# Memory, keys and values of the second block made in front of the first block's experts

## The chip, the cores and the metric

The kernel runs on one core of a Trainium2 chip. The metric is the device time of one execution in microseconds, as the median of several runs. The core's engines are PE (matrix products and transposes), DVE and ACT (element by element work), POOL, and SP, which here only issues loads; ACT and POOL issue loads too. Each engine takes its instructions in the order in which they stand in its own program.

## The reference, cut to what matters

Two blocks follow one another on 256 rows of width 1024, all in 32-bit floats. Of the first block only the second half matters here, of the second block its first lines:

```python
# block 1
x = layer_norm(ALPHA * x + y) * ln1_g + ln1_b            # y: what the mixers gave, through w_out
h = layer_norm(x) * (1 + sc2) + sh2
y = (1 + g2) * hier_moe(h, router_grp_w, router_grp_b, router_exp_w, router_exp_b,
                        exp_w1, exp_w3, exp_w2)           # 32 experts, 2 chosen for each row
x = layer_norm(ALPHA * x + y) * ln2_g + ln2_b
# block 2
p = rms_norm(x, norm_mix_g) @ w_in                        # q is the first part of p
mem_n = rms_norm(mem, norm_mem_g)                         # mem: 256 x 1024, an input
kh, vh = mem_n @ w_mk, mem_n @ w_mv                       # each 256 x 256; don't depend on x
o_att = softmax(q @ kh.T / 8) @ vh                        # by head
```

After that block 2 has its convolution, its RWKV part and 16 experts of its own.

## The kernel before

Rows lie on the 128 partitions in two halves, t = 0 and 1. Block 1's mixers end in `b1_merge` and `b1_out` (product with w_out, residual, moments). `b1_out` frees the tiles of the mixers, opens slots for weights in their place, and starts the stream of the experts: 96 pieces of 2 MB (w1, w3 and w2 of 32 experts), which `fetch` (L1079) loads one after another into nine slots, A0, A1, A2, B0, B1, A3, B2, B3 and S, round and round, on SP's queue. S consists of two halves, which hold LN1's rows `ln1` and the transposed x `HT` until the router is through with them. The first three pieces are fetched in `b1_out`, five in `m1_router`, the ninth behind x's normalization; each later one when the piece nine before it has been used.

`m1_router` (L1100) loads the router's weights into `KmT` and `Vm` (the tiles that later hold block 2's keys and values), its biases into `rbias` and LN1's rows by column into `ln_f`, all in small loads on ACT's queue. `weighted` (L1129) multiplies the weights by four vectors on DVE; `ps_rw` sums them. LN1 and the router's own normalization are folded: `ps_rl` makes the logits from x before LN1 (transposed into HT), and `rlogit` corrects them by means, roots and sums (`rw_col`). Meanwhile DVE normalizes x in place (L1158 and L1159), takes its moments (L138) and roots, ACT writes the normalized rows `z` (L1180), and DVE selects two experts for each row (`sel`). `ps_rank` (L1214) counts the rows ahead of each one, `onehot` places them, `ps_x` (L1276) gathers the rows of four experts, and `ps_h` (L1294) are the first products with the experts' weights.

Behind the last expert `b2_memory` (L1423) loads mem, w_mk and w_mv into slots that the experts have left, transposes mem (`ps_mT`), scales it by column (`nmem`) and makes keys and values (`ps_km`, 32 products with 256 columns). The rows' root mean square is applied later, in `b2_memory_out` (L1459): a product `ps_mr` turns the factors into a row, ACT copies it, DVE multiplies. In between stand LN2 and the mean square of x. Then `b2_in` (L1646) scales x to `z`, transposes it (`ps_z`), ACT and DVE split it into `h_hi` and `h_lo`, and `psd` (L179) is the first product with w_in.

A scheduler that simulates the program puts the instructions of each engine in order. Every load signals its landing on a counter; SP's and ACT's loads go round eight counters, and a load waits in its engine's order until the load before it on its counter has landed. That is the wait DMAHW0 to DMAHW7 in the orders below; POOL's loads go round eight others.

## Time and profile before

| | |
|---|---|
| median of three runs | 1684.29 us (1680.11, 1684.29, 1698.09) |
| profiled execution, its own time | 1693.76 us |
| its span in the trace | 1692.1 us |
| mean granted clock of PE | 0.877 |
| PE / DVE / ACT / POOL busy | 77% / 41% / 20% / 7% |
| bytes read from memory | 507.08 MB |

The span is the profiled execution without what lies around it (1.7 us). The trace counts microseconds from the start of the span. A row of a timeline gives the start, the length, engine, line, operation, what is written and read, and how many instructions were run together; in brackets stands how long the engine sat idle before, and what ended that. SPq and ACTq are the engine's own queue of instructions, in which loads are issued. `wp` is the common name of all the slots' tiles, L62 the line that issues every load. PEclk is the clock that PE was granted, as a share of full speed.

### The profile page before, as it was taken

How to read it: one execution, taken by the hardware profiler on the slowest of the kernel's cores; microseconds unless marked ns; L12 is line 12 of the kernel's file. 1: busy time of each engine (PE TensorE's matmuls, PEld its weight loads, DVE VectorE, ACT ScalarE, POOL GpSimd, SP SyncE). 2: the span in 40 equal slices, each digit the busy share in tenths (PEclk: the TensorE clock that was granted, in tenths of full speed). 3: DMA queues.
4: the chain of work that ended last, by engine and by line, in shares of the span. 5: the costliest groups of instructions: out<-in, count | busy, mean ns of one | idle time of the engine just before them, and what ended most of it. 6: DMA issues, size and time to landing. Idle time of an engine off the chain costs nothing.

```text
span 1692.1 us, 35400 instructions
## 1 busy us (share of the span) xinstructions
PE 1306.0 (77%) x15539; PEld 987.6 (58%) x15539; DVE 695.6 (41%) x1839; ACT 337.3 (20%) x727; POOL 111.4 (7%) x160
## 2 busy tenths in 40 slices
PE   5999999999587775666557998988977766656555
PEld 3898988878565544454435897668853423323222
DVE  4896657687732222122114686465631101001002
ACT  1443433554210000000002453221210000000001
POOL 2122000122000000000000021120000000000000
PEclk9999989899799898898889997675989777878788
DMA  9566578774989999999998611312689999999996
GB/s 330 176 170 143 151 226 259 250 224 166 397 342 424 425 426 426 425 425 426 426 423 309 180 47 35 102 51 94 248 340 422 425 424 426 422 425 425 423 424 263
DMA packets 154947, 513.77 MB, mean 304 GB/s; under 512 B 12319, under 2 KB 118423, under 8 KB 123814
## 3 DMA queue, kind: packets, MB, share of 16 engines
q1 hardware_dynamic: 145152, 499.85, 75.6%
q10 hardware_dynamic: 8886, 10.99, 2.7%
q8 instruction: 124, 2.03, 0.5%
q0 software_dynamic: 752, 0.63, 0.1%
q14 instruction: 33, 0.27, 0.0%
HBM read 507.08 MB, written 2.62 MB: 301 GB/s over the span
## 4 chain that ended last, share of the span: by engine, by line
DMA 49%; PE 37%; DVE 9%; ACT 2%; issue 2%; SPq 1%; POOL 0%; ACTq 0%; DVEq 0%; POOLq 0%
DMA wp<-in_exp_w_dram 21%; PE psd L179 12%; DMA wp<-in_w_e_up_dram 9%; DMA wp<-in_w_e_down_dram 8%; DMA wp<-in_w_e_gate_dram 6%; PE psn L198 4%; PE ps_h L1294 2%; DVE wlo L160 1%; DMA wc<-in_w_in_dram 1%; DMA ada<-in_ada_w_dram 1%; PE ps_x L1276 1%; PE ps_on L880 1%; PE ps_lv L1934 1%; PE ps_cv L1750 1%; SPq L62 1%
## 5 line engine op out<-in xcount | busy, mean ns | idle before, releaser
L2370 PE MATMUL ps_h<-wp,xg 128*32 128x256 f32 x2048 | 160.4, 460 | 98.1 <-DMA wp<-in_w_e_up_dram 57.0
L1294 PE MATMUL ps_h<-wp,xg 128*32 128x128 f32 x4096 | 160.6, 312 | 89.1 <-DMA wp<-in_exp_w_dram 79.9
L1294 PEld LDWEIGHTS ps_h<-wp,xg 128*32 128x32 f32 x4096 | 135.8, 123 | 121.3 <-DMA wp<-in_exp_w_dram 53.8
L2370 PEld LDWEIGHTS ps_h<-wp,xg 128*32 128x32 f32 x2048 | 70.4, 125 | 186.1 <-DMA wp<-in_w_e_up_dram 57.3
L160 DVE TENSOR_TENSOR wlo<-wc,whi 128x1024 fp32r<-128x1024 f32 (+2 forms) x111 | 138.1, 1258 | 49.5 <-ACT whi L159 44.7
L159 ACT CAST whi<-wc 128x1024 fp32r<-128x1024 f32 (+2 forms) x111 | 114.4, 1041 | 141.9 <-PE psd L179 84.0
L179 PE MATMUL psd<-hT_hi,wlo 128*128 128x256 f32 x432 | 124.1, 288 | 3.6 <-DVE wlo L160 3.6
L179 PE MATMUL psd<-hT_hi,whi 128*128 128x256 f32 x432 | 126.1, 292 | 0.0
L179 PE MATMUL psd<-hT_lo,whi 128*128 128x256 f32 x432 | 124.6, 289 | 0.0
L2391 PE MATMUL ps_y<-wp,Vm 128*32 128x256 f32 x960 | 74.8, 470 | 30.5 <-DMA wp<-in_w_e_down_dram 27.4
L1301 DVE SCALAR_TENSOR_TENSOR eu<-eth,ps_h 128x128 f32<-128x128 f32 x32 | 9.2, 286 | 192.7 <-ACT eth L1299 192.7
L179 PEld LDWEIGHTS psd<-hT_hi,wlo 128*128 128x128 f32 x432 | 84.0, 195 | 6.0 <-DVE wlo L160 4.9
L179 PEld LDWEIGHTS psd<-hT_hi,whi 128*128 128x128 f32 x432 | 84.6, 196 | 2.8 <-issue 2.0
L179 PEld LDWEIGHTS psd<-hT_lo,whi 128*128 128x128 f32 x432 | 84.1, 195 | 1.6 <-issue 1.6
L1299 ACT ACTIVATE eth<-ps_h 128x128 f32<-128x128 f32 x32 | 8.9, 277 | 372.0 <-PE ps_h L1294 372.0
L1325 DVE TENSOR_TENSOR ey<-ps_y,mod 32x256 f32<-32x256 f32 x124 | 52.1, 420 | 65.7 <-PE ps_y L1319 64.3
L1319 PE MATMUL ps_y<-wp,egT 128*32 128x256 f32 x992 | 64.5, 401 | 12.8 <-DVE egT L1311 7.3
L2391 PEld LDWEIGHTS ps_y<-wp,Vm 128*32 128x32 f32 x960 | 35.4, 132 | 64.9 <-issue 29.7
L2395 ACT COPY ey<-ps_y 32x256 f32<-32x256 f32 x30 | 10.9, 364 | 289.4 <-DVE ey L2395 289.4
L2395 DVE COPY ey<-ps_y 32x256 f32<-32x256 f32 x30 | 12.5, 418 | 118.5 <-PE ps_y L2391 111.9
L2378 DVE SCALAR_TENSOR_TENSOR KmT<-KmT,ps_h 128x256 f32<-128x256 f32 x16 | 6.7, 422 | 126.8 <-PE ps_h L2370 126.8
L2377 DVE SCALAR_TENSOR_TENSOR KmT<-KmT,ps_h 128x256 f32<-128x256 f32 x16 | 6.7, 422 | 113.1 <-ACT KmT L2375 113.0
(665 smaller groups left out, 2614.2 us busy)
## 6 DMA issues: line engine op xcount, KB each, us to landing
wp<-in_exp_w_dram SPq DMA_DIRECT2D x85, 2048.0 KB, 34.3
wp<-in_w_e_up_dram SPq DMA_DIRECT2D x19, 2048.0 KB, 27.8
wc<-in_w_in_dram SPq DMA_DIRECT2D x35, 1024.0 KB, 5.6
wp<-in_w_e_gate_dram SPq DMA_DIRECT2D x16, 2048.0 KB, 29.0
wp<-in_w_e_down_dram SPq DMA_DIRECT2D x16, 2048.0 KB, 27.0
wp<-in_w_e_down_dram SPq DMA_DIRECT2D x32, 1024.0 KB, 27.1
wp<-in_w_e_gate_dram SPq DMA_DIRECT2D x30, 1024.0 KB, 27.0
wp<-in_w_e_up_dram SPq DMA_DIRECT2D x24, 1024.0 KB, 27.0
```

What stands on the lines that cost most here:

```text
L62: d = (eng or self.nc.sync).dma_start(out=out, in_=in_)
L159: nc.scalar.copy(hi[:, :kk, cs], src)
L160: i = nc.vector.tensor_tensor(lo[:, :kk, cs], src, hi[:, :kk, cs].bitcast(FT), op=OP.subtract)
L179: mm = lambda w, x, st, sp: nc.tensor.matmul(ps[:, c], w, x, start=st, stop=sp, skip_group_check=True)
L198: mm = lambda x, w, st, sp: nc.tensor.matmul(ps[t], x, w, start=st, stop=sp, skip_group_check=True)
L880: mm = lambda t, v, p, st, sp: nc.tensor.matmul(po[:, t], v, p, start=st, stop=sp, skip_group_check=True)
L1294: nc.tensor.matmul(ph[32 * j:32 * j + 32, i].rearrange("p (m c) -> p m c", c=2), xg[:, k, 32 * el:32 * el + 32], v[:, j % 2, j // 2], star ...
L1319: nc.tensor.matmul(py[32 * q:32 * q + 32], gT[j], w2[j][:, 256 * q:256 * q + 256], start=j == 0, stop=j == 3, skip_group_check=True, tile_ ...
L1325: nc.vector.tensor_tensor(Y[32 * el:32 * el + 32, qs], py[32 * q:32 * q + 32], self.g2[32 * el:32 * el + 32, qs], op=OP.mult)
L2370: nc.tensor.matmul(ph[32 * j:32 * j + 32].rearrange("p (m c) -> p m c", c=2), xg[:, 4 * kk + k, 32 * el:32 * el + 32], v[:, j], start=kk + ...
L2391: nc.tensor.matmul(py[32 * q:32 * q + 32], gT[:, c, 32 * j:32 * j + 32], w2[2 * j + c][:, 256 * q:256 * q + 256], start=j + c == 0, stop=j ...
L2395: (nc.scalar.copy if q % 2 else nc.vector.tensor_copy)(Y[32 * el:32 * el + 32, 256 * q:256 * q + 256], py[32 * q:32 * q + 32])
```

## The change

`b1_out` fetches one expert piece in place of three. In front of it `b2_memory_in` takes the first two slots: mem and w_mk go into A0, w_mv and the place for the transposed memory into A1. Its rows are squared on ACT, the roots taken on DVE and the rows scaled on ACT there and then. `m1_router` loads `norm_mem_g` as eight rows, transposes it on PE (`ps_nm`) to have it by column, and makes `ps_mT` and `ps_km` behind the logits; `ps_km` is copied on ACT into KmT and Vm. `ps_km` uses PSUM banks "y" and "x" in place of "h" and "y"; the first four experts' `ps_x` uses bank "x" alone, in place of "x" and "t" by turns. At the end of the experts the loads of the memory, `ps_mT`, `ps_km`, `ps_mr` and DVE's multiplications are gone. The slots' order goes on from two more places.

```diff
@@ -984,8 +984,8 @@
         self.ln1 = self.shaped(self.single("A"), [P, 2, D])
         for i, nm in enumerate(("ln1_g", "ln1_b")):
             self.rows_to_all(self.ln1[:, i], I[nm][0], nc.scalar)
-        for i in range(3):
-            self.fetch()
+        self.b2_memory_in()
+        self.fetch()
         self.close("w1", "ws", "b1t", "b1", "pc", "pd")
 
     def moments_of(self, pool, st, eps, tag):
@@ -1119,6 +1119,12 @@
                                 channel_multiplier=-1)
         self.before = before
         ones = self.ones
+        nm8 = sp.tile([8, P], FT, name="nmem8")
+        self.load(nm8, I["norm_mem_g_2"][0].rearrange("(r p) -> r p", p=P), nc.scalar)
+        pn = self.pm.tile([P, 8], FT, name="ps_nm", tag="x")
+        nc.tensor.transpose(pn, nm8, self.idn[:8, :8])
+        nmem = sp.tile([P, 8], FT, name="nmem")
+        nc.scalar.copy(nmem, pn)
 
         lg1 = sp.tile([P, 2, 8], FT, name="ln1_f")
         for i, nm in enumerate(("ln1_g", "ln1_b")):
@@ -1154,6 +1160,7 @@
             self.transpose_rows(self.pm, x[:, t], HT, t, ("t", "x"), eng=nc.scalar.copy)
             for k in range(8):
                 nc.tensor.matmul(pl[:, t], HT[:, k, t * P:(t + 1) * P], rs_[:, k], start=k == 0, stop=k == 7)
+        self.b2_memory(nmem)
         for t in range(2):
             nc.vector.scalar_tensor_tensor(x[:, t], x[:, t], mv[t][:, 0:1], lnp[:, 0], op0=OP.subtract, op1=OP.mult)
             nc.vector.scalar_tensor_tensor(x[:, t], x[:, t], rs[t], lnp[:, 1], op0=OP.mult, op1=OP.add)
@@ -1267,9 +1274,9 @@
             if el == 0:
                 G = self.one_hot(e)
                 xg = self.mt.tile([P, 8, P], FT, name="xg", tag="xg")
-                n = 4 if e else 2
+                n = 4
                 for c0 in range(0, 8, n):
-                    px = self.pm.tile([P, n, P], FT, name="ps_x", tag="x" if e else "xt"[c0 // 2 % 2])
+                    px = self.pm.tile([P, n, P], FT, name="ps_x", tag="x")
                     for k in range(n):
                         for t in range(2):
                             c = c0 + k
@@ -1349,15 +1356,13 @@
                     self.rows_to_all(r, I[nm][0])
             self.b2_early(e)
         self.inorder = False
-        kv = self.b2_memory()
         mv = [self.moments_of(self.kv, st[t], 1e-5, f"a{t}") for t in range(2)]
         rs = self.rsqrts(self.kv, [m[:, 1:2] for m in mv], ["ar0", "ar1"], self.LN2LAG)
         for t in range(2):
             nc.vector.scalar_tensor_tensor(x[:, t], x[:, t], mv[t][:, 0:1], lnp[0], op0=OP.subtract, op1=OP.mult)
             nc.vector.scalar_tensor_tensor(x[:, t], x[:, t], rs[t], lnp[1], op0=OP.mult, op1=OP.add)
         self.dump("x2", x)
-        self.rsx = self.mean_square(self.kv, x, "nx", self.shaped(self.free[3], [P, D]))
-        self.b2_memory_out(*kv)
+        self.rsx = self.mean_square(self.kv, x, "nx", self.shaped(self.halves(self.slot(self.spare))[0], [P, D]))
 
     E_IF = 29
     LN2LAG = 0
@@ -1366,6 +1371,7 @@
 
         nc, I, tc = self.nc, self.I, self.tc
         n = nc.values_load(self.cnt[0:1, 0:1], min_val=0, max_val=T)
+        self.spare = self.order[self.npiece % len(self.order)]
         HT = self.big([P, 8, T], name="ov_hT")
         ws = self.big([P, 2, 8, P], name="ov_w")
         w2g = self.big([P, 2, D], name="ov_wg")
@@ -1420,52 +1426,43 @@
         if e == 5:
             self.b2_vectors()
 
-    def b2_memory(self):
-
-        nc, sp = self.nc, self.m1
-
-        o = self.order
-        m, (wk, wv), self.free = self.slot(o[8])[0], self.halves(self.slot(o[2])), \
-            self.halves(self.slot(o[0])) + self.halves(self.slot(o[1]))
-        mT = self.free[0]
-        m = m.rearrange("p (t d) -> p t d", t=2)
-        wk, wv, mT = [w.rearrange("p (k n) -> p k n", k=8) for w in (wk, wv, mT)]
+    def b2_memory_in(self):
+
+        nc = self.nc
+        (m, wk), (wv, mT) = [self.halves(self.take()) for _ in range(2)]
+        jk = self.shaped(mT, [P, 2, D])
+        self.mem = m = m.rearrange("p (t d) -> p t d", t=2)
+        self.mem_w = wk, wv = [w.rearrange("p (k n) -> p k n", k=8) for w in (wk, wv)]
+        self.memT = mT.rearrange("p (k n) -> p k n", k=8)
         self.load(m, self.I["mem_2"][0].rearrange("(t p) d -> p t d", p=P))
         for w, nm in ((wk, "w_mk_2"), (wv, "w_mv_2")):
             self.load(w, self.I[nm][0].rearrange("(k p) n -> p k n", p=P))
+        rs = self.mean_square(self.b1, m, "mm", [jk[:, t] for t in range(2)])
+        for t in range(2):
+            nc.scalar.activation(m[:, t], m[:, t], AF.Copy, scale=rs[t])
+
+    def b2_memory(self, nmem):
+
+        nc, m, mT, (wk, wv) = self.nc, self.mem, self.memT, self.mem_w
         for k2 in range(4):
             ps = self.pm.tile([P, 2, T], FT, name="ps_mT", tag="tx"[k2 % 2])
             for a in range(2):
                 k = 2 * k2 + a
                 for t in range(2):
-                    nc.tensor.transpose(ps[:, a, t * P:(t + 1) * P], m[:, t, k * P:(k + 1) * P], self.idn)
+                    i = nc.tensor.transpose(ps[:, a, t * P:(t + 1) * P], m[:, t, k * P:(k + 1) * P], self.idn)
+                    if k + t == 0:
+                        self.tc.keep_in_program_order(i)
             for a in range(2):
                 k = 2 * k2 + a
-                nc.scalar.activation(mT[:, k], ps[:, a], AF.Copy, scale=self.v2["nmem"][:, k:k + 1])
-        out = []
+                nc.scalar.activation(mT[:, k], ps[:, a], AF.Copy, scale=nmem[:, k:k + 1])
         for v in range(2):
-            ps = self.pm.tile([P, 2, T], FT, name="ps_km", tag="hy"[v])
+            ps = self.pm.tile([P, 2, T], FT, name="ps_km", tag="yx"[v])
             for a in range(2):
                 s = slice(a * P, (a + 1) * P)
                 for k in range(8):
                     l, r = (mT[:, k, s], wv[:, k]) if v else (wk[:, k, s], mT[:, k])
                     nc.tensor.matmul(ps[:, a], l, r, start=k + a == 0, stop=k == 7, skip_group_check=True)
-                out.append(ps[:, a])
-
-        rs = self.mean_square(self.kv, m, "mm", self.shaped(self.free[1], [P, D]))
-        pr = self.pm.tile([P, T], FT, name="ps_mr", tag="t")
-        return out, rs, pr
-
-    def b2_memory_out(self, km, rs, pr):
-        nc = self.nc
-        for t in range(2):
-            nc.tensor.matmul(pr[:, t * P:(t + 1) * P], rs[t].to_broadcast([P, P]), self.idn, start=t == 0, stop=True,
-                             skip_group_check=True)
-        row = self.shaped(self.free[2], [P, T])
-        nc.scalar.copy(row, pr)
-        for a in range(2):
-            nc.vector.tensor_tensor(self.KmT[:, a], km[a], row, op=OP.mult)
-            nc.vector.tensor_scalar(self.Vm[:, a], km[2 + a], rs[a], None, op0=OP.mult)
+            nc.scalar.copy(self.Vm if v else self.KmT, ps)
 
     def b2_vector_loads(self):
         I = self.I
@@ -1538,7 +1535,7 @@
             ss = sp.tile([P, 1], FT, name="ms_s", tag=f"{tag}s{t}")
             r = sp.tile([P, 3], FT, name="rs_y", tag=f"{tag}y{t}")
             out.append(r[:, 0:1])
-            nc.scalar.activation(jk, x[:, t], AF.Square, accum_out=ss)
+            nc.scalar.activation(jk[t] if isinstance(jk, list) else jk, x[:, t], AF.Square, accum_out=ss)
             nc.vector.tensor_scalar(ss, ss, 1.0 / D, 1e-6, op0=OP.mult, op1=OP.add)
             yield
             yield from self.rsqrt_steps(ss, r)
```

The scheduler moves instructions with this. On ACT, before, the router's loads stood between the last work of the mixers (`onT_hi`) and the casts of the weights for the merge; this is that place, around `b1_merge`:

```order
L145 CAST onT_hi<-ps_on 128x256 [waits PE_49]
L62 DMA KmT<-in_router_grp_w_dram 128x8x4 [waits DMAHW3_49]
L62 DMA KmT<-in_router_exp_w_dram 128x8x32
L62 DMA rbias<-in_router_grp_b_dram 128x4
L62 DMA rbias<-in_router_exp_b_dram 128x32
L159 CAST whi<-wc 128x1024 [waits PE_49]
L62 DMA ln_f<-in_ln_g_dram 128x8
L62 DMA ln_f<-in_ln_b_dram 128x8 [waits DMAHW0_49]
```

In the change they stand behind the scaling of the memory's rows, after the last cast and the first copies into HT, and behind them come the rest of HT's copies and everything that ACT does in the router:

```order
L1442 ACTIVATE wp<-wp,rs_y 128x1024 [waits DVE_49,Activation_49] x2
L62 DMA KmT<-in_router_grp_w_dram 128x8x4 [waits DMAHW1_49]
L62 DMA KmT<-in_router_exp_w_dram 128x8x32 [waits DMAHW2_49]
L62 DMA rbias<-in_router_grp_b_dram 128x4 [waits DMAHW3_49]
L62 DMA rbias<-in_router_exp_b_dram 128x32 [waits DMAHW4_49]
L62 DMA nmem_4928<-in_norm_mem_g_dram 8x128 [waits DMAHW5_49]
L62 DMA ln_f<-in_ln_g_dram 128x8 [waits DMAHW6_49]
L62 DMA ln_f<-in_ln_b_dram 128x8 [waits DMAHW7_49]
L1127 COPY nmem<-ps_nm 128x8 [waits PE_49]
L1009 COPY wp<-ps_tr 128x4x128 [waits PE_49] x2
L1457 ACTIVATE wp<-ps_mT,nmem 128x256 [waits PE_49,Activation_49]
```

The seven loads moved from ahead of the merge's last casts to behind them; each now waits on one counter, and the counters 1 to 7 are in order those of w_mv and of the first six expert pieces.

On PE, in the router, from the logits to the gather of the first rows, before:

```order
L1156 MATMUL ps_rl<-Vm,wp 128x36 [waits Activation_49]
L1156 MATMUL ps_rl<-Vm,wp 128x36 x3
L1214 MATMUL ps_rank<-sel,before 128x32 [waits DVE_49]
L1215 MATMUL ps_rank<-sel,before 128x32
L1216 MATMUL ps_rank<-sel,ones 128x32
L1222 MATMUL ps_cnt<-sel,ones 1x32 [waits PE_49]
L1222 MATMUL ps_cnt<-sel,ones 1x32
```

And in the change, from the first product of keys and values on:

```order
L1464 MATMUL ps_km<-wp 128x256 [waits DMAHW7_49,DVE_49,Activation_49]
L1464 MATMUL ps_km<-wp 128x256 [waits DMAHW1_49]
L1452 MATMUL ps_mT<-idn,wp 128x128 [waits PE_49,Activation_49]
L1452 MATMUL ps_mT<-idn,wp 128x128 x3
L1464 MATMUL ps_km<-wp 128x256 x6
L1464 MATMUL ps_km<-wp 128x256 [waits Activation_49]
L1464 MATMUL ps_km<-wp 128x256
L1464 MATMUL ps_km<-wp 128x256 [waits Activation_49]
L1464 MATMUL ps_km<-wp 128x256 x21
L1221 MATMUL ps_rank<-sel,before 128x32 [waits DVE_49]
```

All 32 products `ps_km`, with the last four transposes `ps_mT` between them, stand between the logits and `ps_rank`. The first of them waits for the DVE copy `rw_col`, whose bank it takes.

On DVE, in the change, from the router's four multiplications `weighted` to x's normalization (before, the multiplications stood among the splits of the merge, long ahead of this):

```order
L1136 TENSOR_TENSOR Vm<-KmT,sh_3003 128x288 [waits DMAHW2_49,DMAHW1_49]
L1137 TENSOR_REDUCE rw_sum<-Vm 128x36 [waits DVE_49]
L1136 TENSOR_TENSOR KmT<-KmT,sc_3004 128x288
L1137 TENSOR_REDUCE rw_sum<-KmT 128x36 [waits DVE_49]
L1136 TENSOR_TENSOR Vm<-KmT,ln_f 128x288 [waits DMAHW7_49]
L1165 SCALAR_TENSOR_TENSOR x<-x,bn_mv,wp 128x1024 [waits DMAHW5_49,PE_49]
L1137 TENSOR_REDUCE rw_sum<-Vm 128x36 [waits DVE_49]
L1166 SCALAR_TENSOR_TENSOR x<-x,rs_y,wp 128x1024 [waits DMAHW0_49,DVE_49]
```

The third multiplication, which waits for counter 7, the last `ln_f`, moved ahead of x's first operation.

## Rows read from the trace of the kernel before

**Rows 1.** Page: DMA share of 40 slices; the chain that ended last.

```profile
DMA  9566578774989999999998611312689999999996
...
DMA 49%; PE 37%; DVE 9%; ACT 2%; issue 2%; SPq 1%; POOL 0%; ACTq 0%; DVEq 0%; POOLq 0%
```

**Rows 2.** Busy time by stretch (window, length, busy by engine, granted PEclk, DMA share, GB/s).

```profile
445.00:459.00 14.00, 0.12 (x1) 0.12 (x1) 12.92 (x62) 4.11 (x4) 0.00 (x0) 0.51 1.00 422
459.00:465.00 6.00, 5.44 (x30) 5.00 (x34) 2.88 (x15) 0.46 (x1) 0.00 (x0) 0.50 0.96 399
465.00:473.00 8.00, 8.00 (x130) 6.47 (x134) 2.12 (x7) 1.74 (x4) 0.00 (x0) 0.96 0.06 24
520.00:905.00 385.00, 256.27 (x4674) 185.45 (x4668) 82.44 (x240) 20.41 (x56) 1.38 (x5) 0.88 1.01 424
930.00:940.00 10.00, 7.31 (x39) 6.21 (x38) 5.85 (x13) 3.00 (x5) 0.29 (x1) 1.00 1.06 288
```

**Rows 3.** Waits of SP's queue, 520 to 905 (total us, times, longest).

```profile
SPq L62 <- DMA wp<-in_exp_w_dram: 316.2, 79, 6.1
```

**Rows 4.** SP issues (start, length); the issue at 437.64: KB, us to landing.

```profile
430.46 7.51 SPq L62 DMA_DIRECT2D wp<-in_exp_w_dram  x5
...
472.41 2.14 SPq L62 DMA_DIRECT2D wp<-in_exp_w_dram  x2
...
wp<-in_exp_w_dram SPq DMA_DIRECT2D x1, 2048.0 KB, 24.2
```

**Rows 5.** POOL and ACT issuing small loads (idle before and its releaser); one load's landing.

```profile
424.31 0.50 POOL L62 DMA_DIRECT2D raw<-in_iclr_a_dram  x1 [1.66 <-DMA raw<-in_norm_mix_g_dram]
...
401.29 1.06 ACT L159 CAST whi<-wc 128x1024 fp32r<-128x1024 f32 x1 [2.50 <-DMA KmT<-in_router_grp_w_dram]
...
ln_f<-in_ln_g_dram ACTq DMA_DIRECT2D x1, 4.0 KB, 2.7
```

**Rows 6.** The router on DVE, PE and ACT, by timeline.

```profile
408.03 0.45 DVE L1130 TENSOR_TENSOR Vm<-KmT,ln_f 128x288 f32<-128x288 f32 x1
...
410.13 0.68 DVE L1131 TENSOR_REDUCE rw_sum<-Vm 128x36 f32<-128x288 f32 x1
...
443.59 2.48 DVE L1158 SCALAR_TENSOR_TENSOR x<-x,bn_mv,wp 128x1024 f32<-128x1024 f32 x2
445.98 2.48 DVE L1159 SCALAR_TENSOR_TENSOR x<-x,rs_y,wp 128x1024 f32<-128x1024 f32 x2
448.37 2.47 DVE L138 BATCH_NORM_STATS2 bn_st<-x 128x6 f32<-128x512 f32 x4
...
453.13 0.25 DVE L1169 SCALAR_TENSOR_TENSOR rlogit<-rlogit,rs_y,rbias 128x36 f32<-128x36 f32 x1
...
458.61 0.22 DVE L1206 TENSOR_TENSOR sel<-fm_eq 128x64 f32<-128x64 f32 x1
...
458.88 0.64 PE L1214 MATMUL ps_rank<-sel,before 128*128 128x32 f32 x2 [16.00 <-DVE sel L1206]
...
461.24 3.75 PE L1276 MATMUL ps_x<-onehot,mod 128*128 128x128 f32 x16 [0.56 <-DVE onehot L1233]
...
454.24 3.99 ACT L1180 ACTIVATE mod<-x,nmrs,rs_y 128x1024 f32<-128x1024 f32 x2
```

**Rows 7.** End of the stream: PE, ACT, DVE; the 64 records of L1452.

```profile
913.24 3.67 PE L1261 MATMUL acc<-ey,ecw 128*128 128x512 f32 x8
...
922.92 12.68 PE L1452 MATMUL ps_km<-wp 128*128 128x256 f32 x58
...
938.78 0.38 PE L179 MATMUL psd<-h_hi,whi 128*128 128x256 f32 x1 [1.86 <-ACT h_hi L1663]
...
936.09 0.37 ACT L1465 COPY wp<-ps_mr 128x256 f32<-128x256 f32 x1 [7.37 <-PE ps_mr L1462]
...
929.52 0.75 DVE L1652 TENSOR_SCALAR z<-x,rs_y 128x1024 f32<-128x1024 f32 x1
...
L1452 PE MATMUL ps_km<-wp x64: 379/379/454, 920.7 to 935.2; 128*128 128x256 f32 x64
```

## The prediction

> **What bounds the kernel now.** I read the page first, then busy time by stretch, then the waits of the SP queue, then the timelines of single engines around the two places that the change touches. All times are microseconds from the start of the profiled execution.
>
> The page's row of DMA shares stands at 9 through two long runs of slices, and the chain that ended last is 49% DMA [rows 1]. Between 520 and 905 the DMA is busy all the time at 424 GB/s while PE works 256 of 385 us [rows 2]: block 1's experts are a stream, one 2 MB piece per 2.097 MB / 424 GB/s = 4.95 us. A stream like this ends as late as it was held up before, so what counts is when it stands still. It stands still once: from 465 to 473 the DMA share is 0.06 [rows 2]. Nine pieces have been issued by then, one for each slot, and the tenth can be issued only when the first expert product has freed a slot, at 472.41 [rows 4]. What sets that moment is the router: x normalized on DVE from 443.59, statistics, selection until `sel` at 458.61, then PE's `ps_rank`, which had sat idle 16.00 us, `ps_x` at 461.24 and the expert products [rows 6]. So the date to follow is that of the tenth piece.
>
> The second place is the end of this stream. PE works on the memory's keys and values from 920.7 to 935.6 (`ps_km`, 64 records, the last 58 of them in 12.68 us), and block 2's first product `psd` comes at 938.78 [rows 7], although its input `z` was on its way at 929.52 [rows 7].
>
> **The change, part by part.**
>
> *The load in front.* Memory, w_mk and w_mv are 3.15 MB, 7.4 us at 424 GB/s. They take two slots, which before took two pieces (9.9 us), and those pieces come later through the same two slots. Nine expert pieces have been issued in both kernels before the tenth, so the 7.4 us is no further term as long as the tenth is what decides; it is the whole cost if the tenth were not delayed (rivals).
>
> *The router's small loads on ACT's queue.* This is the step on which the forecast rests. Before, they stood ahead of the merge's last casts and one of those casts followed them at 401.29 [rows 5]. Now the order puts them behind the memory's squares and scaling, and each waits for an earlier load on its counter: the router's weights for w_mv and for the first expert piece, the biases for the second and third, `nmem` for the fourth, the last of them (`ln_f`, LN1's bias) for the sixth. The trace shows what such a wait is. SP stood 316.2 us in 79 waits of this kind [rows 3], and POOL, issuing small loads one after another, stood 1.66 us until the load eight earlier had landed [rows 5]. An engine waits in order: ACT's cast at 401.29 came 2.50 us late behind its loads [rows 5]. So ACT stands until the sixth piece has landed, and behind it are queued `nmem`, the copies of the second half of HT, `ps_mT`'s scaling, `gexp` and `z`. On DVE the third `weighted` needs that last `ln_f` and stands ahead of the first `x` operation, so x's normalization waits too.
>
> When is that? Before, the eighth piece was issued at 437.64 and took 24.2 us, so it landed at 461.8 [rows 4]. Now 3.15 MB and six pieces are ahead, in place of eight pieces: 1.05 MB less, 2.5 us earlier, 459.3; but the second expert piece still waits for a DVE operation of the merge, as at 430.46 [rows 4], and the queue can run dry ahead of it. I take 460.5 (459.3 to 461.8). `ln_f` then takes 2.7 us to land, as before [rows 5], and 0.4 to issue: 463.6. POOL's small loads took longer beside full queues, but here nothing else is in flight, since the next piece (the ninth slot's first half) waits for x. At the upper end I allow 3 us more.
>
> *DVE from there.* Two `weighted` (0.45 each, and a reduction of 0.68 behind each), the x operations 2.48 + 2.48, statistics 2.47, reciprocal roots 2.6 (450.8 to 453.4, the last logits), and 0.4 for the router's sums: 12.9 us [rows 6]. That is 476.4, against 453.4 in the profile. From there to `sel` it was 5.2 us (453.4 to 458.61), and some 1.0 more goes to the logits' first four operations, which stood ahead of x before (0.25 each, as at 453.13): 483 [rows 6].
>
> *Keys and values in front of `ps_rank`.* In PE's new order all 32 products stand ahead of `ps_rank`. The first needs the PSUM bank that `rw_col` frees at about 476; the rest need the last scaled transposes, which ACT has queued behind `gexp` and two `z` operations (3.99 us together [rows 6], where the tile goes by `mod`), so they come at about 483 to 485. About eight products fit in before that, 24 are left. One costs two records, 12.68/58 x 2 = 0.437 us, at the full clock [rows 7]: 10.5 us, until 494. The clock is open: PE's granted clock was 0.51 from 445 to 459, when it had nothing to do, and 0.50 until 465 [rows 2], and PE now idles from 443 to about 476. At the half clock throughout it is 32 x 0.874 = 28 us from 476, until 504. I take the full clock for the 24, since PE was back at 0.96 in 465 to 473 after some 7 us of work [rows 2].
>
> *From `ps_rank` to the tenth piece.* Before, 2.4 us to `ps_x` and 11.2 to the issue, at the half clock until 465; without it I take 1.7 and 9. So 494 + 10.7 = 504.7 against 472.4: **+32 us**, between +27 (early landing, K and V done by 490) and +45 (half clock, late landing). The two slots of the memory come free a little before that and are the eighth and ninth piece; they fill part of the hole, but the tenth still waits.
>
> The Trainium skill says ("DMA: Bandwidth & Descriptors", Rules for kernel authors) to issue a DMA early, compute, and wait on its semaphore late. That speaks for this change as a whole; what it would give here is the first rival. The same page (Issuing engines are not separate DMA queues) counts only the sequencer's time for starting a load and calls it usually small; by that alone ACT's seven loads would cost some 4 us. SP's and POOL's rows above disagree: the issuing engine's stand is the length of an earlier transfer.
>
> *The end of the stream.* `ps_km`, `ps_mr` and the row scaling are gone there. ACT waited 7.37 us for `ps_mr` before it made the casts and `h_hi` [rows 7]; without it the path is z (929.52 + 0.75), transposes, `h_hi`, `psd` at about 931.5, in place of 938.78: -7 us. DVE loses the steps of one pair of roots, up to -1.5 more; two of the loads ahead of w_in_2 are gone (2.1 MB, 7 us at the 288 GB/s of 930 to 940 [rows 2]), so weights don't hold it. On the other side PE comes to block 2 colder. -5 to -10, I take **-7**.
>
> *At no cost:* `ps_nm`, the squares of the memory (ACT was free), the junk slot's new place, `ps_x` with one bank in place of two for the first four experts.
>
> Sum: +32 - 7 = **+25 us**. The profiled execution took 1693.8; the median of the three runs is 1684.3, and they lie 18 us apart. On the median's footing I expect **1709**.
>
> **The rivals.**
>
> *A, the other side: the router is not held up.* If ACT's loads ran ahead (their counters free in time), x and the selection keep their dates, K and V fit into PE's 16 us of idle time and the 7.4 us of loading into the 8 us hole at 465. Then the end's gain is left: -7, up to -9: about 1676. For it: hole and idle time are there [rows 2]. Against it: the order's waits name pieces that land after 450. It decides if x's normalization starts before about 448.
>
> *B, the router is late but K and V are cheap.* If landing comes at 457 and PE is warm, the tenth piece is at 490 to 494: +18 to +21, less 7 to 10: +10 to +13, 1695 to 1697, within 1%. Against it: the products cannot begin before `rw_col`.
>
> *C, half clock.* K and V at 0.874 us throughout, and slow small loads: the tenth at 515 to 518, +43 to +45, less 7: 1720 to 1722. For it: the clock row of 445 to 465.
>
> **How the numbers follow.** A difference of 1% is about what a measurement of this kernel can tell, so slower means above 1701, faster below 1667. Forecast (+17 to +31, 1701 to 1715) 0.58, C (up to 1724) 0.17, B 0.14, A 0.11. A's gain is 0.5%, and only its upper part passes 1%: faster 0.04. Same: the rest of A and B, and the forecast's lower edge: 0.21. Slower 0.75. The range reaches from B's lower end to above C, 1692 to 1724, and leaves out A and a little beyond C.
>
> **What would show it.** Right: ACT issues the last `ln_f` after 459 and computes nothing just before; DVE has a wait for `ln_f` of some 15 us and x starts near 464; `ps_rank` stands behind `ps_km` and comes near 494; the DMA is idle in about 460 to 472, again around 480 to 490, and the tenth expert piece is issued near 505; the last piece lands near 937; from `acc` to the first `psd` it is 7 us less than before (913.24 to 938.78 [rows 7]). Wrong: x starting before 450 (A), K and V over by 490 (B), a granted clock of 0.5 through all of them (C), or a first `psd` no nearer to `acc`, when another wait has taken the place of `ps_mr`.

## The result, and the profile after

| | before | after |
|---|---|---|
| median | 1696.85 us (5 runs, 1680.11 to 1698.09) | 1708.39 us (5 runs, 1699.24 to 1712.39) |
| ratio to before | 1 | 1.0114 (95%: 1.0067 to 1.0162), some 19 us (11 to 27) |
| profiled execution, span | 1692.1 us | 1697.5 us |
| granted clock of PE, mean | 0.877 | 0.866 |

The change makes the kernel slower by about 1%. The profiled execution of after is the fastest of its five, so its span stands only 5.4 us above that of before; the stages tell more than the span.

The page of after, DMA share of 40 slices and the chain that ended last (it answers to [rows 1]):

```profile
DMA  9556478775759999999999541302679999999997
...
DMA 22%; PE 16%; DVE 5%; SPq 1%; ACT 1%; issue 1%; ACTq 0%; DVEq 0%
```

A slice is 42 us. In the two slices from about 424 to 508 the share is 7 and 5, where it was 9 and 8, and the long run of nines behind them ends one slice later. Busy time by stretch (window, length, PE, PEld, DVE, ACT, POOL, granted PEclk, DMA share, GB/s; it answers to [rows 2]):

```profile
459.00:465.00 6.00, 3.63 (x13) 2.34 (x13) 5.93 (x9) 1.85 (x5) 0.00 (x0) 0.50 0.01 1
465.00:473.00 8.00, 7.62 (x36) 7.62 (x37) 7.14 (x32) 1.17 (x3) 0.00 (x0) 0.50 0.40 131
473.00:480.00 7.00, 6.44 (x26) 5.30 (x26) 5.37 (x30) 5.02 (x6) 0.00 (x0) 0.63 0.46 152
480.00:485.00 5.00, 5.00 (x25) 4.41 (x24) 1.12 (x8) 0.71 (x4) 0.00 (x0) 1.00 0.00 0
490.00:495.00 5.00, 4.17 (x34) 3.66 (x32) 2.47 (x12) 0.82 (x2) 0.00 (x0) 1.00 0.97 393
520.00:905.00 385.00, 272.97 (x4782) 196.78 (x4777) 85.31 (x250) 22.54 (x61) 0.00 (x0) 0.84 1.01 425
```

The hole of 8 us in [rows 2] has become a stretch of 26 us in which the DMA is idle or half busy. Why, the timelines of ACT and DVE show:

```profile
441.59 13.16 ACTq L62 DMA_DIRECT2D rbias<-in_router_grp_b_dram  x1
...
457.53 0.44 ACTq L62 DMA_DIRECT2D ln_f<-in_ln_b_dram  x1
459.46 0.17 ACT L1127 COPY nmem<-ps_nm 128x8 f32<-128x8 f32 x1 [17.91 <-PE ps_nm L1125]
```

```profile
458.63 0.46 DVE L1136 TENSOR_TENSOR Vm<-KmT,sh 128x288 f32<-128x288 f32 x1 [16.44 <-DMA KmT<-in_router_exp_w_dram]
...
461.08 1.28 DVE L1165 SCALAR_TENSOR_TENSOR x<-x,bn_mv,wp 128x1024 f32<-128x1024 f32 x1
...
481.07 0.22 DVE L1213 TENSOR_TENSOR sel<-fm_eq 128x64 f32<-128x64 f32 x1
...
491.76 0.23 DVE L1225 SCALAR_TENSOR_TENSOR rank<-ps_rank,sel 128x64 f32<-128x64 f32 x1 [9.86 <-PE ps_rank L1223]
```

ACT stands 13.16 us on one small load. DVE waits 16.44 us for the router's weights, which ACT issued at 440.83, ahead of that stand; a second wait of 9.86 us is for PE, busy with keys and values. The weights' load itself was slow. Issues of after between 430 and 465 (KB each, us from issue to landing):

```profile
wp<-in_exp_w_dram SPq DMA_DIRECT2D x3, 2048.0 KB, 20.0
...
KmT<-in_router_exp_w_dram ACTq DMA_DIRECT2D x1, 128.0 KB, 17.7
```

Why it was slow, the packets show in which the loads move (queue: packets, MB, share of the DMA engines' time; q1 carries SP's loads, q10 ACT's). The first two rows are 444 to 454, the last two 456 to 458:

```profile
q1 hardware_dynamic: 292, 4.26, 99.5%
q10 hardware_dynamic: 285, 0.00, 1.6%
...
q10 hardware_dynamic: 1942, 0.16, 73.7%
q1 hardware_dynamic: 48, 0.13, 17.0%
```

ACT's seven loads are 2,672 packets, most of them of 16 or 128 bytes; SP's pieces go in packets of mostly 16 KB. From 444 to 454 about one packet of ACT's went for each one of SP's, some 29 in a microsecond. When SP's last piece was through, 1,942 went in 2 us.

ACT's stand is not the wait for a completion counter that the prediction names. The load ahead on the counter of the load that stood, the second expert piece, had landed at 436.6 by the trace, 5 us before the stand began; the four loads behind it found their counters free too (landed 441.5, 446.4, 451.4 and 456.4; issued 454.8, 455.4, 456.6 and 457.5). What lay ahead of that load were the packets of ACT's first two loads, in its own queue. That the queue had no room for more is likely, but no run shows it.

PE and SP, from there to the tenth piece:

```profile
459.16 0.27 PE L1125 MATMUL ps_nm<-idn,nmem 8*128 8x8 f32 x1 [23.61 <-DMA nmem<-in_norm_mem_g_dram]
...
477.84 13.29 PE L1464 MATMUL ps_km<-wp 128*128 128x256 f32 x60
490.97 0.30 PE L1221 MATMUL ps_rank<-sel,before 128*128 128x32 f32 x2
...
492.49 2.02 PE L1283 MATMUL ps_x<-onehot,mod 128*128 128x128 f32 x16 [0.56 <-DVE onehot L1240]
```

```profile
501.16 2.15 SPq L62 DMA_DIRECT2D wp<-in_exp_w_dram  x2
```

The end of the stream, on PE (it answers to [rows 7]):

```profile
942.91 3.67 PE L1268 MATMUL acc<-ey,ecw 128*128 128x512 f32 x8
...
961.72 0.58 PE L179 MATMUL psd<-h_hi,whi 128*128 128x256 f32 x1
```

From `acc` to the first `psd` it is 18.8 us, where it was 25.5.

**How the traces are compared.** Executions differ ahead of the changed place: the first transpose of x (`ps_tr`) came at 436.41 in the profile of before and at 432.43 in a second profile of the same kernel. So all times below are counted from that transpose, and the span is cut at two more places: the first `psd` of block 2, and the first product of block 2's own router, `ps_rl` with `r_last`. Between these two lies block 2's mixing work (its RWKV part above all), behind them the experts of block 2. Nothing in either part was edited.

| kernel | `ps_rank` | tenth piece | first `psd` | against before | mixing | rest |
|---|---|---|---|---|---|---|
| before | 22.5 | 36.0 | 502.4 | | 287.5 | 465.8 |
| x9, before again | 22.5 | 36.0 | 502.2 | -0.2 | 287.6 | 464.4 |
| after | 58.0 | 68.1 | 528.7 | +26.3 | 275.9 | 459.9 |
| x5, after again | 57.7 | 67.9 | 528.5 | +26.1 | 275.9 | 459.9 |
| x2, before without the memory | 22.5 | 36.0 | 496.3 | -6.0 | 289.8 | 460.6 |
| x4, slot, few products | 26.5 | 36.9 | 499.3 | -3.0 | 276.9 | 460.4 |
| x1, slot | 34.0 | 44.2 | 504.8 | +2.4 | 287.8 | 461.3 |
| x8, slot and POOL | 34.0 | 44.2 | 504.8 | +2.4 | 277.3 | 460.5 |
| x7, slot and order | 35.4 | 45.6 | 506.2 | +3.8 | 286.8 | 460.3 |
| x6, loads on POOL | 41.0 | 51.2 | 511.6 | +9.2 | 276.0 | 459.8 |
| x3, few products | 48.4 | 60.9 | 523.5 | +21.1 | 287.5 | 460.5 |

From the tenth piece to the first `psd` it is 466.4 and 466.2 us in the two profiles of before, and 460.3 to 460.6 in seven of the others (462.4 and 462.6 in x4 and x3). So for those seven the loss at the first `psd` is the delay of the tenth piece less 6 us for the end of the stream.

Up to the first `psd` the change costs 26.3 us. Then two stretches give back 11.6 and 5.9, which leaves 8.8 of this pair of executions.

### The profile page after: what moved, and what is told of

It is laid out like the page before. It is cut to its first block, busy times and chain, and to the rows that moved or that the text cites. A ratio compares the mean times of both kernels' runs of the same rounds, so it can differ in the third digit from the quotient of the medians.

```text
span 1697.5 us, 35396 instructions
## 1 busy us (share of the span) xinstructions
PE 1311.5 (77%) x15536; PEld 983.9 (58%) x15536; DVE 693.5 (41%) x1835; ACT 340.8 (20%) x731; POOL 114.2 (7%) x160
## 5 line engine op out<-in xcount | busy, mean ns | idle before, releaser
L1301 PE MATMUL ps_h<-wp,xg 128*32 128x128 f32 x4096 | 168.3, 319 | 79.9 <-DMA wp<-in_exp_w_dram 66.2
L160 DVE TENSOR_TENSOR wlo<-wc,whi 128x1024 fp32r<-128x1024 f32 (+2 forms) x111 | 141.7, 1289 | 49.8 <-ACT whi L159 43.9
L2388 PE MATMUL ps_y<-wp,Vm 128*32 128x256 f32 x960 | 73.5, 465 | 27.1 <-DMA wp<-in_w_e_down_dram 23.9
L1326 PE MATMUL ps_y<-wp,egT 128*32 128x256 f32 x992 | 75.0, 450 | 14.9 <-DMA wp<-in_exp_w_dram 10.6
L1326 PEld LDWEIGHTS ps_y<-wp,egT 128*32 128x32 f32 x992 | 36.7, 126 | 40.6 <-issue 20.0
L2375 DVE SCALAR_TENSOR_TENSOR KmT<-KmT,ps_h 128x256 f32<-128x256 f32 x16 | 6.7, 421 | 126.8 <-PE ps_h L2367 126.8
```

The costliest lines, as they stand in the source:

```text
L160: i = nc.vector.tensor_tensor(lo[:, :kk, cs], src, hi[:, :kk, cs].bitcast(FT), op=OP.subtract)
L1301: nc.tensor.matmul(ph[32 * j:32 * j + 32, i].rearrange("p (m c) -> p m c", c=2), xg[:, k, 32 * el:32 * el + 32], v[:, j % 2, j // 2], star ...
L1326: nc.tensor.matmul(py[32 * q:32 * q + 32], gT[j], w2[j][:, 256 * q:256 * q + 256], start=j == 0, stop=j == 3, skip_group_check=True, tile_ ...
L2388: nc.tensor.matmul(py[32 * q:32 * q + 32], gT[:, c, 32 * j:32 * j + 32], w2[2 * j + c][:, 256 * q:256 * q + 256], start=j + c == 0, stop=j ...
```

## The experiments

The theory was that of the prediction: the seven small loads, late in ACT's order, hold ACT, and DVE with it; keys and values in front of `ps_rank` hold the tenth piece further. The rivals: the 7.4 us of loading in front, or the products alone, make the loss. In the kernels with the slot edit, line numbers are 9 higher than in after (up to 17 in x7).

**x1: the memory's roots in the slot.** Only the place of four small tiles changes. They leave the pool of the mixers, and the scheduler puts the router's loads back among the merge's casts.

```diff
-        rs = self.mean_square(self.b1, m, "mm", [jk[:, t] for t in range(2)])
+        rs = self.mean_square(Cut(jk[:, 1]), m, "mm", [jk[:, 0], jk[:, 0]])
```

(`Cut` hands out columns of the slot where the pool handed out tiles.)

> One edit to the changed kernel: the memory's roots (and the junk of its squares) lie in the memory's own slot, no longer in the pool of block 1 over which the router's weight tiles are laid. By the order the seven small loads then stand among the merge's casts again; the 32 products for keys and values stay ahead of ps_rank. Theory (late small loads hold the router, and after that the products hold ps_rank): x starts near 440 in place of 461, sel comes near 457, the products end between 470 and 478 since the last scaled transposes wait behind z and PE is cold, the tenth expert piece is issued at 480 to 488 in place of 501.2; time 13 to 21 us less than the changed kernel, 0 to +7 against the kernel before. Rival (the loads don't matter, the 3.1 MB in front do): time as the changed kernel, +19 against before. Rival (products are free once the router is in time): tenth near 469, -7 against before.

Measured: 1688.13 against 1691.36, ratio 0.9993 (0.9956 to 1.0030). The loads are issued from 393 on, x's normalization starts at 435.1, and the products end at 465.5, somewhat earlier than expected:

```profile
397.12 0.36 ACTq L71 DMA_DIRECT2D ln_f<-in_ln_b_dram  x1
```

```profile
453.35 12.35 PE L1473 MATMUL ps_km<-wp 128*128 128x256 f32 x56 [1.55 <-ACT wp L1466]
465.54 0.30 PE L1230 MATMUL ps_rank<-sel,before 128*128 128x32 f32 x2
```

The same 128 KB of weights now land after 2.8 us:

```profile
KmT<-in_router_exp_w_dram ACTq DMA_DIRECT2D x1, 128.0 KB, 2.8
...
q10 hardware_dynamic: 2387, 0.17, 39.1%
```

The second row is ACT's queue from 394 to 398, with nothing of SP's beside it. The tenth piece comes at 475.7, ahead of the expected 480 to 488. At the first `psd`, 23.9 of the 26.3 us are gone with the place of seven loads. That is the larger part of the loss, shown by undoing it.

**x2: before without the memory.** Loads, products and scaling of the memory are left out; keys and values are a constant.

```diff
-        self.load(m, self.I["mem_2"][0].rearrange("(t p) d -> p t d", p=P))
...
+        self.nc.gpsimd.memset(self.KmT, 0.01)
+        self.nc.gpsimd.memset(self.Vm, 0.01)
```

> The kernel before without the memory's part at the end of the experts: mem, w_mk and w_mv are not loaded, nothing of keys and values is made (both tiles are filled with a constant on POOL). So it leaves out the keys and values. Theory: from acc to the first psd 18.5 to 20 us in place of 25.5, and the time is 7 us less than before (5 to 10). Rival (the end of the stream is bound by the weights of w_in_2 or by DVE): no gain.

Measured: ratio 0.9972 (0.9942 to 1.0002), which just reaches 1. The first `psd` comes 6.0 us earlier:

```profile
911.87 3.67 PE L1261 MATMUL acc<-ey,ecw 128*128 128x512 f32 x8
...
930.63 0.58 PE L179 MATMUL psd<-h_hi,whi 128*128 128x256 f32 x1
```

From `acc` to `psd` it is 18.8 us, as in after. So this is all that moving the memory away from the end can bring.

**x3 and x4: 4 of the 32 products**, in after and in x1. The other 28 are left out, so keys and values are sums over an eighth of the columns.

```diff
-                for k in range(8):
+                for k in range(7, 8):
```

> The changed kernel with 4 of the 32 products for keys and values (one of eight parts of the width; the rest of the sum is left out). Loads, transposes and copies stay. Theory (the products hold ps_rank from 481.7 to 491): ps_rank near 482, the tenth expert piece near 491 to 493 in place of 501.2, time 8 to 10 us less than the changed kernel, +9 to +11 against before. Rival (the two pieces that go into the memory's slots fill the hole, and PE's products are hidden): time as the changed kernel, +19 against before.

> Both edits together: roots in the memory's slot, and 4 of the 32 products (the rest of the sum is left out). What is left of the change is the 3.1 MB in front, the transposes and their scaling. Theory (the load in front is no term of its own): ps_rank near 459 to 462, the tenth expert piece at 470 to 475, and against the kernel before only the gain at the end is left, -5 to -7 us. Rival (the load in front costs its 7.4 us): the tenth may be early, but the time is that of the kernel before, 0 to +2.

Measured, x3: ratio 1.0108 (1.0071 to 1.0145), no less than after's, where 8 to 10 us less were expected. `ps_rank` comes 9.6 us earlier, the tenth piece 7.2, the first `psd` 5.2. Part of the gain goes at once, since PE is idle before `ps_rank` and its clock falls; the same 16 gathers take 3.60 us, where after has 2.02:

```profile
486.01 0.64 PE L1221 MATMUL ps_rank<-sel,before 128*128 128x32 f32 x2 [3.91 <-DVE sel L1213]
...
488.27 3.60 PE L1283 MATMUL ps_x<-onehot,mod 128*128 128x128 f32 x16 [0.47 <-DVE onehot L1240]
```

```profile
485.00:491.00 6.00, 4.52 (x23) 4.27 (x23) 3.10 (x18) 0.63 (x3) 0.00 (x0) 0.50 1.00 429
```

In this profile, the slowest of x3's ten executions, the rest of it goes in the mixing stretch, 287.5 us in place of 275.9; that stretch has two lengths, whatever the edit (last section). The two intervals of after and x3 are too wide to tell a gain of 5 us from none.

Measured, x4: ratio 0.9961 (0.9928 to 0.9994), the time that was expected, but with the short mixing stretch in its profile; first `psd` 5.4 us earlier than in x1. Both pairs price the 28 products at about 5 us at the end of the stream. And x4 stands 3.0 us above x2, where the theory had nothing. From its first transpose to the tenth piece the DMA has no hole any more (columns as above; DMA share 1.01, where [rows 2] has 0.06 in one stretch):

```profile
434.60:471.50 36.90, 22.62 (x190) 17.83 (x192) 24.74 (x124) 16.81 (x29) 0.00 (x0) 0.77 1.01 426
```

So once the router is in time, the load in front can count. How much of the 3.0 us is the load and how much the transposes, the scaling and the four products, these runs don't show: 0.9 stand at the tenth piece, 2.1 behind it, and x3, whose DMA does have a hole, loses 2.0 there too.

**x5: after again, unchanged.**

> The changed kernel once more, not a word different, for a second profile and a second interval. In its first profile block 2 ran some 12 us faster than in the profiles of before and of three of the other kernels, in a stretch (its RWKV part, 1150 to 1220) whose instructions the change does not touch and where PE's granted clock was 0.92 in place of 0.64. If that is chance, this profile may show either, the stage of block 1's experts again starts some 32 us late (68 us from the first transposes of x to the tenth piece, 36 in the kernel before), and the time is +15 to +27 against before. If the change itself makes that stretch faster, the gain is there again and the time is +8 to +16.

Measured: 1704.03 against 1683.73, ratio 1.0130 (1.0085 to 1.0176). All stages repeat within 0.3 us (table). The short mixing stretch is there again, yet the time is not the +8 to +16 us that was expected for this case: 1.3% are 22 us.

**x6: the seven small loads on POOL's queue**, all else as in after.

```diff
-        self.load(rw[:, :, 0:4], I["router_grp_w"][0].rearrange("(p k) n -> p k n", p=P), nc.scalar)
+        self.load(rw[:, :, 0:4], I["router_grp_w"][0].rearrange("(p k) n -> p k n", p=P), nc.gpsimd)
...
```

> The changed kernel with the seven small loads issued by POOL in place of ACT. They still can't be issued before the memory's rows are scaled (their tiles lie over the roots' pool), but they don't wait on the counters of SP's and ACT's loads, and ACT does not stand. Theory (of the 18 us by which x starts late, some 3 are the place in the order and the rest the counters): x starts about 450 in place of 461, limited by 5 to 10 us of landing beside full queues; from the first transposes of x to the tenth piece 56 to 60 us in place of 68; time 8 to 12 us less than the changed kernel, +7 to +12 against before. Rival (the place in the order is all): x at 458 or later, time as the changed kernel.

Measured: 1684.82, ratio 0.9997 (0.9963 to 1.0030), a larger gain than expected. A premise of the expectation was wrong: POOL did not wait for the scaling of the memory's rows, it issued all seven from 419 on:

```profile
423.45 0.54 POOL L62 DMA_DIRECT2D ln_f<-in_ln_b_dram  x1
```

```profile
445.88 0.46 DVE L1136 TENSOR_TENSOR Vm<-KmT,sh 128x288 f32<-128x288 f32 x1
```

The first `weighted` comes at 445.88 with nothing to wait for but DVE's own order (it stands behind the memory's roots, the first of which waited 2.69 us for ACT's squares). So the tiles that the loads fill were free long before; what made them late in after was their place in ACT's order. On POOL's queue (q0) the loads are also fewer packets; from 422 to 433 it moved 368, those of POOL's other loads among them, and the weights landed 8.1 us after their issue, beside SP's pieces:

```profile
q0 software_dynamic: 368, 0.19, 7.0%
...
KmT<-in_router_exp_w_dram POOLq DMA_DIRECT2D x1, 128.0 KB, 8.1
```

17.1 of the 26.3 us go with the move to POOL. How much of it is the earlier issue and how much the other queue, this run doesn't part.

**x7: the slot, and ACT's order pinned.** x1, with the copies into HT held behind the scaling of the memory's rows and `gexp` behind the last scaled transpose.

```diff
-            self.transpose_rows(self.pm, x[:, t], HT, t, ("t", "x"), eng=nc.scalar.copy)
+            self.transpose_rows(self.pm, x[:, t], HT, t, ("t", "x"), eng=self.after_scaled)
...
-        nc.scalar.activation(ge, ge, AF.Exp)
+        self.behind(nc.scalar.activation(ge, ge, AF.Exp), self.turned)
```

> The first experiment's edit (roots in the memory's slot) and two edges in ACT's order: the copies of the transposed x stand behind the scaling of the memory's rows, and gexp and z stand behind the last scaled transposes. So the products for keys and values should run in PE's idle time before ps_rank. Theory: the products end at 458 to 462 (on the axis of the first experiment 465.5), from the first transposes of x to the tenth piece 37 to 41 us (44 there, 36 before), and the time is 2 to 5 us less than the kernel before. Rival (holding ACT's copies back delays the router as much as the products gain): 44 us or more, time as the first experiment, 0 to -2 against before.

Measured: ratio 1.0019 (0.9989 to 1.0050). The rival held. The scaling itself comes late, and the logits behind it:

```profile
443.78 2.19 ACT L1451 ACTIVATE wp<-wp 128x1024 f32<-128x1024 f32 x2 [10.97 <-DVE wp L131]
```

`ps_rank` comes 1.4 us later than in x1.

**x8: slot and POOL together, and x9: before again.**

> The memory's roots in the slot and the seven small loads on POOL's queue together. Theory (the delay of the change is the place of these loads in ACT's order, and either edit alone removes it as far as it can be removed): the loads' queue brings nothing more once the roots stand in the slot, because there ACT's loads stand among the merge's casts again. From the first transpose of x to the tenth piece 44.2 us as with the slot alone (43 to 46), the first psd within 2 us of that kernel's, time ratio to the kernel before 0.998 (0.995 to 1.002). Rival (ACT's loads among the casts cost something there too: the cast at 401.29 had stood 2.50 us behind them in the trace of the kernel before): the first transpose of x comes 2 to 3 us earlier, the whole is 2 to 3 us faster than with the slot alone, ratio about 0.997.

> The kernel before, unchanged, for a second profile of it. Question: whether the RWKV stretch of block 2 (1150 to 1220), which the change does not touch and which was 12 us shorter in the change's two profiles at a higher granted clock, is always long in the kernel before. If its length goes with the program, this profile shows the granted clock of about 0.64 there again and a span of about 1692; if it varies from execution to execution, the stretch may be 12 us shorter and the span about 1680, which is as far below as the fastest of the three runs shown of the kernel before (1680.11).

Measured, x8: 1680.58 against 1692.65, ratio 0.9966 (0.9934 to 0.9999). Up to the first `psd` it is x1 to 0.1 us, as the theory said: the other queue adds nothing where the loads are early. Its ratio is that of the rival, but not for the rival's reason (the first transpose came no earlier, 433.17 against 431.53): its profile has the short mixing stretch, 277.3 us. It is the only complete kernel here whose interval lies below 1, and only just; its 0.3% lie in stretches that the edit does not touch. x9, one profile of 1688.42: the long mixing stretch again, 287.6.

## Why the prediction was right, step by step

The forecast was +25 us and 1709; measured are 1708.39, and 19 us (11 to 27) or, with x5, 1.3% (0.85 to 1.76). That the numbers agree to a microsecond is partly luck: the forecast stood on a median of three, 1684.29, and five runs gave 1696.85. What can be held against its steps is the trace; after's times have 3.4 us to be added (433.02 for 436.41) for the axis of before.

- *ACT held by its small loads, the dates*: right. Forecast: last `ln_f` issued after 459, x from 464; measured 457.53 + 3.4 = 460.9 and 461.08 + 3.4 = 464.5.
- *The same, the cause*: wrong. The prediction had ACT stand on completion counters until the sixth piece had landed. The trace has no such wait: each counter was free when the turn of its load came, and ACT stood 13.16 us on its third load behind its own queue of small packets. Two more profiles say the same: in x5 the stand of 12.82 us began at 440.4, and the counter had been free since 435.4; in x3 12.43 us from 446.3, free since 440.8. The dates agree because the small packets got through when SP's last piece was through, and this is the sixth, landed at 456.4, at which the prediction had its counters end. That is luck, as far as the cause goes. Had the queue been free, the counters would have held ACT's last load until that landing too, so for ACT no run parts the two. For DVE the trace does: it waited not for `ln_f`, as forecast, but in the first `weighted` for weights issued before ACT stood, which were 17.7 us on the way beside three 2 MB pieces (2.8 us in x1) and landed at 458.5. ACT's stand shows on PE, which stood idle 23.61 us until `nmem` had come, with the second half of HT's transposes behind it. x1 and x6 take both away, since there the loads are issued some 20 us and more earlier, from 419 in x6 and from 393 in x1. One row was read wrongly: ACT's cast at 401.29 [rows 5] had not waited for a counter but for the starts of four loads, 398.4 to 401.0. The seven starts took ACT 17.8 us, from 440.16 to 457.96. The Trainium skill ("DMA: Bandwidth & Descriptors", Issuing engines are not separate DMA queues) counts the sequencer's time for starting a load and calls it usually small; this trace disagrees.
- *DVE from there*: `sel` forecast at 483, measured 481.07 + 3.4 = 484.5. It didn't matter, since PE was not free.
- *Keys and values in front of `ps_rank`*: right, 494 forecast, 490.97 + 3.4 = 494.4 measured, with the half clock (0.50) until 473 and the full clock from 480. Rival C is out: the clock was 1.00 from 480 to 495. What this step missed: without the products the clock would be low at `ps_x` (x3), so at the end of the stream they cost 5 us and not the 9.6 by which 28 of them delay `ps_rank`.
- *Tenth piece*: +32 forecast, 68.1 - 36.0 = +32.1 measured.
- *Load in front at no further cost*: right for after, where the router is the later one: from the tenth piece to the first `psd` it is 460.6 us, as in x2 (460.3), which has no such load. It holds only as long as the DMA has a hole ahead of the tenth piece: x4, which has none, stands 3.0 us above x2.
- *End of the stream*: -7 forecast, 18.8 - 25.5 = -6.7 measured; x2 shows the same alone.
- *Sum up to block 2*: +25 forecast, +26.3 and +26.1 measured. By parts, each the difference of two kernels at the first `psd`: -6.0 for the memory gone from the end (x2), +3.0 for what the change puts in front, with four products (x4 less x2), +5.4 for the products (x1 less x4), +23.9 for the late small loads (after less x1).
- *Nothing behind it*: wrong, and the one term that the sum lacked. The experts of block 2 take about 5 us less in all nine profiles of kernels without the memory's loads at the end of block 1's stream, and the mixing stretch 11.6 us less in both profiles of after. The measured +19 lies between the +26 at the first `psd` and the +9 that the two profiles show at the end (1697.5 - 433.02 and 1696.1 - 431.82, against 1692.1 - 436.41). The mixing stretch looks like chance (last section); without its part the pair of profiles would stand at 26.3 - 5.9 = +20.4, an estimate that agrees with the medians.

Rival A fell with x's date. Its 1676 supposed that the router could be in time at no cost; x1, where x starts 3.6 us behind the first transpose (7.2 in before), still has the tenth piece 8.2 us later than before, and the end gives back only 6.0. Rival B's sum, redone, is +8 to +14 (18 - 10 to 21 - 7), not +10 to +13; nothing hangs on it.

## What to carry to other kernels

A small load that comes to stand beside large ones is late twice: on its way (17.7 us for 2.8), since its small packets go one for each large packet of the other queue, and in what its engine does next, since the next load on the same queue could not be started for 13.16 us and all that is queued behind it waits. When large loads are moved ahead, look first at which small loads now come beside them, and how many packets each of them is; here the place of seven of them was worth 24 us, while 3.15 MB in front, with the transposes and four products, cost 3 us even where the router was in time (x4). And a neutral or better variant can differ in four small tiles: read the order that comes out, not the edit.

## What was not expected of the hardware

The mixing stretch of block 2 has two lengths in the eleven profiles, 276 to 277 us and 287 to 290 us. In all of them PE's granted clock falls to 0.50 after PE was idle for 2.0 us (at 1141.5 in before, at 1164.3 in after), and what differs is when it comes back. Windows of before and x9 (columns as above):

```profile
1144.00:1150.00 6.00, 5.95 (x80) 5.46 (x76) 5.78 (x16) 1.35 (x3) 0.00 (x0) 0.50 0.51 175
...
1174.00:1180.00 6.00, 6.00 (x61) 5.81 (x63) 1.25 (x5) 0.58 (x1) 0.00 (x0) 0.50 0.03 11
1186.00:1192.00 6.00, 6.00 (x69) 5.37 (x68) 4.98 (x22) 1.63 (x2) 0.00 (x0) 1.00 0.23 98
```

```profile
1144.00:1150.00 6.00, 3.94 (x54) 3.45 (x50) 5.92 (x22) 2.53 (x7) 0.00 (x0) 0.50 0.01 3
...
1174.00:1180.00 6.00, 6.00 (x67) 5.90 (x67) 1.87 (x6) 0.00 (x0) 0.00 (x0) 0.50 0.37 116
```

And of after and x8:

```profile
1174.00:1180.00 6.00, 4.77 (x54) 4.31 (x56) 4.90 (x16) 2.60 (x5) 0.00 (x0) 0.50 0.15 29
1186.00:1192.00 6.00, 6.00 (x84) 5.41 (x85) 2.75 (x10) 1.54 (x3) 1.34 (x2) 1.00 0.43 143
```

```profile
1150.00:1156.00 6.00, 3.25 (x40) 2.76 (x40) 5.62 (x20) 3.08 (x6) 0.00 (x0) 0.50 0.00 0
1162.00:1168.00 6.00, 5.74 (x103) 5.09 (x100) 3.37 (x13) 1.65 (x4) 1.34 (x2) 1.00 0.16 35
```

The clock stays at 0.50 for 44 us in the six profiles with the long stretch and for 17 us in the five with the short one. In the six it fell 1.7 to 2.0 us after the idle time began, in the five 2.2 to 2.3; whether this decides is open. Two profiles of the same kernel agreed both times (before and x9, after and x5), but the times speak for chance of the single execution: the profiles with the short stretch are the fastest of their kernel's executions in after, x5 and x4, the one of x3, with the long stretch, is the slowest of its ten, and the twelve times of x8 fall into two groups, seven from 1675.9 to 1682.3 and five from 1686.6 to 1692.2. It is of the size of the whole effect measured, so a difference of 0.5% between two variants of this kernel can come from there.

Block 2's expert stream ran at 424 GB/s in both profiles of before and at 428 or 429 in the nine others, after among them:

```profile
1300.00:1600.00 300.00, 198.44 (x2146) 97.99 (x2146) 28.00 (x69) 12.97 (x35) 0.00 (x0) 0.82 1.01 428
```

x2, which only lacks the memory's part, has it too, so it isn't the memory's new place; what makes the difference was not tried.
